# Last MLP: two blocks of k instead of one in the seven-product form, for the first pair of down chunks of each quarter

## The chip, the cores and the metric

The kernel runs on one core of one Trainium2 chip. Its engines work side by side, each through its own list of instructions in order, and wait for each other by semaphores: TensorE (PE; its weight loads are shown as PEld), VectorE (DVE), ScalarE (ACT), GpSimd (POOL), and SyncE (SP), which here issues the loads of weights. Matrix products are summed in PSUM, in banks of 128 x 512 fp32; all other tiles lie in SBUF. The metric is the device time of one execution in microseconds; less is better.

## The reference

Two layers, each a token mixer, a cross-attention to a memory and a squared-ReLU MLP, with plain residual adds, on 256 tokens of width 2048 in fp32. What matters here is the MLP of the second layer, the last one, which the final norm follows:

```python
D_MODEL = 2048; SEQ = 256; D_FF = 4 * D_MODEL

def squared_relu_mlp(h, w_up, w_down):
    return jnp.square(jax.nn.relu(h @ w_up)) @ w_down
...
x = x + squared_relu_mlp(rms_norm(x, g_ff[i]), f_w_up[i], f_w_down[i])
...
return rms_norm(x, g_final)
```

`w_up` is 2048 x 8192, `w_down` 8192 x 2048.

## The kernel before

Every fp32 operand of a large product is split into a high part (`hi`, rounded by ACT to the format that PE reads) and a low part (`lo`, the rest, by a subtraction on DVE); `split` does both. A product of two tiles is then three matmuls: high x high, low activation x high weight, high activation x low weight.

Weights come in tiles of two k tiles by 512 columns (128 x 1024 fp32 on chip, 512 KB). `wload` has SP load one into a ring of four raw tiles `wraw`; `wtile` splits it into a ring of three tiles `whi` and a ring of three `wlo` (pool `wp`). So casting and splitting can run ahead of PE by three tiles at most, loads by four raw tiles more.

The last MLP (`mlp` with `nxt.closing`) goes through four quarters of the 8192 hidden features. Each quarter `b` has an up stage, four chunks `n` of 512 features made by two calls of `gemm_feat` each (32 weight tiles in all); the result `r` (squared ReLU) is split into `hh` and `hl`. Then comes a down stage: 16 k tiles of the hidden features by the four chunks of 512 output columns. In the first three quarters chunks 0 and 1 are one pair, 2 and 3 another; in the last quarter only 0 and 1 are a pair, chunk 2 goes through `gemm_hid` and chunk 3 through `gemm_last`, which takes both buffers of the pool `act`.

A pair goes through `gemm_seven`. It sees four k tiles as a 2 x 2 block matrix: two blocks of two k tiles by two chunks, and on the other side two halves of 128 tokens by the two blocks of k. Instead of eight block products it makes seven, from sums and differences of blocks. Those of the weights are made by DVE (into `run`, and into one raw tile) and then split; those of the hidden features (`sums`) are made once a quarter by `token_sums` from the first up chunk, and serve both pairs. The remaining twelve k tiles, six weight tiles for each of the two chunks, are direct tiles: each is used for both halves of tokens, 12 matmuls. A product of the seven takes 6 matmuls. Direct tiles stand between the products (`whole`), so that DVE can keep up.

The four raw tiles of the block lie in a ring `ws` of four; the split parts of the four summed products lie in two tiles `own`, one high and one low, all other parts in the ring `whi`/`wlo`. The products go to four PSUM banks, (token half, chunk). Some of them are needed in two places: `keep` has ACT copy a bank to an SBUF tile `kept` while the bank goes on summing. These copies are `m5` and `m1` early, `u2` and `u3` later; `gather` adds them to `x` on DVE.

The order of instructions on each engine is fixed when the program is built: a scheduler follows the program order as priority and takes what it expects to be ready first. SBUF buffers of a pool are taken when free; a new tile waits for the last reader of the one before it.

Lines used below: 103 and 104 are the cast and the subtraction of `split`, 127 the load of `wload`, 174 and 179 the matmuls of `gemm_feat` (high and low weights), 190 and 191 its way out of PSUM, 649 the squared ReLU, 666 `gather`, 697 to 700 `token_sums`, 719 the loads of the block, 731 the matmul in `gemm_seven`, 763 `keep`, 771, 777, 782 and 787 the differences of weights, 791 the sum of `u3` and `m5`.

Of the kernel before, what the change touches and what calls it, by code (L numbers as in the profile page):

```python
# [9 lines left out]
F32 = mybir.dt.float32  # L10
F32R = mybir.dt.float32r
I32 = mybir.dt.int32
AF = mybir.ActivationFunctionType
ALU = mybir.AluOpType
AX = mybir.AxisListType

P = 128
D = 2048
S = 256
KT = D // P  # L20
NB = 512
NCH = D // NB
KB = 2
# [15 lines left out]
class Trunk:  # L39
# [454 lines left out]
    def attention(self, x, layer, cur, nxt):  # L494
        nc, a, tc = self.nc, self.a, self.tc
        wq, wk, wv, wo = (a[k][layer] for k in ("x_w_q", "x_w_k", "x_w_v", "x_w_o"))
        hT = cur.act
        with tc.tile_pool(name="at", bufs=2, reuse_waits="tile") as ap:
# [3 lines left out]
            memT = self.mem_prep(ap, layer)  # L502
# [44 lines left out]
            for hd in range(HEADS):  # L547
                q = proj(hT, wq, hd, "q")
                self.flush()
                k = proj(memT, wk, hd, "k", (1, 2, 3, 0))  # L550
# [6 lines left out]
            oT = self.new_act()  # L557
            homes = iter(("vh", "vl") * 2 + ("ql", "qh") * 6)
            ws = lambda: ap.tile([P, KB * NB], F32, name="ws", tag=next(homes))
# [6 lines left out]
            def values(h0):  # L566

                vs, more = [], {}

                def end(t, n, src):  # L570
                    if not vs:
                        vs.extend([ap.tile([P, 2, HD], F32R, name=nm) for nm in ("vh", "vl")] for _ in range(2))
                    part = more.pop((t, n), None)
                    if part is not None:
                        nc.vector.tensor_tensor(out=part, in0=src, in1=part, op=ALU.add)
                        src = part
                    vh, vl = (f[:, t, :] for f in vs[n - h0])
                    r = self.rstd_mem[:, t:t + 1]
                    nc.scalar.activation(out=vh, in_=src, func=AF.Copy, scale=r)
                    nc.vector.scalar_tensor_tensor(out=vl, in0=src, scalar=r, in1=vh.bitcast(F32),  # L580
                                                   op0=ALU.mult, op1=ALU.subtract)

                self.gemm_seven(tiles, token(memT), self.mem_sums, wv, h0, 0,
                                lambda t, n, part: more.update({(t, n): part}), end)
                return vs

# [35 lines left out]
                nc.vector.tensor_tensor(out=xc, in0=part, in1=xc, op=ALU.add)  # L622

            for j in range(0, NCH, 2):
                self.gemm_seven(tiles, token(oT), sums[0], wo, j, 0, gather)
                for n in (j, j + 1):
                    self.at(1 + n - j, lambda n=n: nxt.chunk(x, n))


    def mlp(self, x, layer, cur, nxt):  # L630
        nc, a, tc = self.nc, self.a, self.tc
        wu, wd = a["f_w_up"][layer], a["f_w_down"][layer]
        hT = cur.act
        with tc.tile_pool(name="ml", bufs=4, reuse_waits="tile") as mp:
            r2 = mp.tile([P, 32 if layer else 56], F32, name="r2", bufs=1)[:, 0:2]
            ws = lambda: mp.tile([P, KB * NB], F32, name="ws", bufs=4)
            run = lambda: mp.tile([P, KB * NB], F32, name="run", bufs=1)
            kept = lambda i: mp.tile([P, NB], F32, name="kept", bufs=4)
            self.fifth = None if nxt.closing else mp
            for b in range(DFF // D):  # L640
                hid = []
                for n in range(NCH):
                    h = mp.tile([P, 4, S], F32R, name="hh")
                    l = mp.tile([P, 4, S], F32R, name="hl")
                    rs = []
                    for i in range(2):
                        r = mp.tile([P, 2, S], F32, name="r", bufs=2)
                        self.gemm_feat(hT, wu, 2 * (NCH * b + n) + i, r)
                        nc.vector.scalar_tensor_tensor(out=r, in0=r, scalar=0.0, in1=r, op0=ALU.max, op1=ALU.mult)
                        self.split(h[:, 2 * i:2 * i + 2], l[:, 2 * i:2 * i + 2], r)  # L650
                        rs.append(r)
                    hid.append((h, l))
                    if nxt.closing and n == 0:
                        sums = self.token_sums(ws(), lambda: mp.tile([P, 4, 2, P], F32R, name="sums", bufs=2), *rs)
                if nxt.closing:
                    own = lambda: mp.tile([P, KB * NB], F32R, name="own", bufs=2)
                    nxt.room = lambda: mp.tile([P, 2, NB], F32, name="g", tag="ws", bufs=4)
                if b == 0:
                    rstd = cur.rstd()
                    nc.vector.tensor_tensor(out=r2, in0=rstd, in1=rstd, op=ALU.mult)  # L660
                if b == DFF // D - 1 and not nxt.closing:
                    nxt.start()

                def gather(t, n, part, cs=None):
                    xc = x[:, t, cs or slice(n * NB, (n + 1) * NB)]
                    nc.vector.scalar_tensor_tensor(out=xc, in0=part, scalar=r2[:, t:t + 1], in1=xc,
                                                   op0=ALU.mult, op1=ALU.add)

                for n in range(NCH):
                    end = b == DFF // D - 1  # L670
                    if nxt.closing and not (end and n >= NCH - 2):
                        if n % 2 == 0:
                            self.gemm_seven((ws, run, kept), lambda kt, t: [f[:, kt % 4, t * P:(t + 1) * P]
                                                                            for f in hid[kt // 4]],
                                            sums, wd, n, b * KT, gather, own=own)
                            if end:
                                nxt.start()
                    elif nxt.closing and end and n == NCH - 1:
                        self.gemm_last(hid, wd, n, b * KT, lambda t, acc: nxt.finish(x, t, lambda cs: gather(
                            t, n, acc[:, cs.start - n * NB:cs.stop - n * NB], cs)))  # L680
                        break
                    else:
                        acc = self.gemm_hid(hid, wd, n, b * KT)
                        for t in range(2):
                            gather(t, n, acc[:, t, :])
                    if end:
                        self.at(4 + n if nxt.closing and n < 2 else 1, lambda n=n: nxt.chunk(x, n))

            self.fifth = None
# [12 lines left out]
        self.split(sh, sl, s)  # L702
        return sh, sl

    def gemm_seven(self, tiles, token, sums, w, n0, k0, gather, end=None, own=None):

# [13 lines left out]
        def parts(src, own=None):  # L722
            hi, lo = (own() if own else self.wp.tile([P, KB * NB], F32R, name=nm) for nm in ("whi", "wlo"))
            self.split(hi, lo, src)
            return half(hi), half(lo)

        begun = set()

        def into(key, kts, left, hi, lo, end=False):
            out = banks[key]  # L730
            mm = lambda s, m, e: nc.tensor.matmul(out, s, m, start=key not in begun, stop=e, skip_group_check=True)  # L731
            for kk in kts:
                ah, al = left(kk)
                mm(ah, hi[:, kk, :], False)
                begun.add(key)
                mm(al, hi[:, kk, :], False)
            for kk in kts:
                mm(left(kk)[0], lo[:, kk, :], True)

        def block(key, t, i, src, end=False):  # L740
            into(key, range(KB), lambda kk: token(KB * i + kk, t), *parts(src), end)

        def summed(key, k, src, end=False):
            into(key, range(KB), lambda kk: [f[:, k, kk, :] for f in sums], *parts(src, own), end)

        todo = {j: list(range(2, KT // KB)) for j in range(2)}

        def direct(j, first):

# [18 lines left out]
        for i, j in ((0, 0), (0, 1), (1, 0), (1, 1)):  # L768
            fetch(i, j)
        run = run()  # L770
        v.tensor_tensor(out=run, in0=raw[0, 1], in1=raw[0, 0], op=ALU.subtract)
        summed((0, 1), 0, run, True)
        block((1, 0), 0, 0, raw[0, 0], True)
        m5, m1 = keep((0, 1), 0), keep((1, 0), 1)
        block((0, 0), 0, 1, raw[1, 0])
        whole(1, 1)
        v.tensor_tensor(out=run, in0=raw[1, 1], in1=run, op=ALU.subtract)
        summed((1, 0), 1, run, True)
        gather(0, n0, m1)
        u2 = keep((1, 0), 2)  # L780
        whole(1, 1)
        v.tensor_tensor(out=raw[0, 1], in0=raw[1, 1], in1=raw[0, 1], op=ALU.subtract)
        summed((1, 0), 2, raw[0, 1], True)
        gather(0, n0 + 1, u2)
        u3 = keep((1, 0), 3)
        whole(0, 0)
        v.tensor_tensor(out=run, in0=raw[1, 0], in1=run, op=ALU.subtract)
        block((1, 0), 1, 1, run)
        whole(1, 1)
        summed((0, 1), 3, raw[1, 1])  # L790
        v.tensor_tensor(out=u3, in0=u3, in1=m5, op=ALU.add)
        whole(0, 0)
        gather(1, n0 + 1, u3)
# [749 lines left out]
```

## Time and profile before

| | us |
|---|---|
| runs: median of 3 (lowest, highest) | 2790.95 (2790.82, 2792.07) |
| the profiled execution: its time | 2789.63 |
| its span, first to last instruction | 2787.9 |
| last MLP, first quarter: up stage begins | about 2083 |
| down stages of quarters 1 to 3: begin | 2170.5, 2344.4, 2518.2 |
| last quarter: pair begins, and `gemm_hid` after it | 2692.1, 2734.3 |

All times of the profile are counted from its first instruction. A share of busy time is an average over stages with different limits, so the stages are read one by one: the chain of work that ended last shows, step by step back from the end, what each step waited for; the view by stretches gives each engine's busy time between two points of time; the waits show which engine waited for which, and for how long; the timeline gives single instructions (start, length, engine, line, operation, output and inputs, and in brackets the idle time before it with what ended it). The length that is shown for a matmul is longer than the distance to the next one, because matmuls overlap.

### The profile page before, as it was taken

How to read it: one execution, taken by the hardware profiler on the slowest of the kernel's cores; microseconds unless marked ns; L12 is line 12 of the kernel's file. 1: busy time of each engine (PE TensorE's matmuls, PEld its weight loads, DVE VectorE, ACT ScalarE, POOL GpSimd, SP SyncE). 2: the span in 40 equal slices, each digit the busy share in tenths (PEclk: the TensorE clock that was granted, in tenths of full speed). 3: DMA queues.
4: the chain of work that ended last, by engine and by line, in shares of the span. 5: the costliest groups of instructions: out<-in, count | busy, mean ns of one | idle time of the engine just before them, and what ended most of it. 6: DMA issues, size and time to landing. Idle time of an engine off the chain costs nothing. (4 is left out here: it accounts for less than half of the span.)

```text
span 2787.9 us, 39690 instructions
## 1 busy us (share of the span) xinstructions
PE 2767.1 (99%) x15020; PEld 2331.6 (84%) x15020; DVE 1984.8 (71%) x2740; ACT 1396.2 (50%) x1805; POOL 234.4 (8%) x435
## 2 busy tenths in 40 slices
PE   9999999999999999999999999999999999999998
PEld 7888888888888888888887888888888888888887
DVE  6865756778978778787567657557776767667665
ACT  6545544554534434444556445445554545445454
POOL 0100000001022222221213100000000000000000
PEclk9999999999999999999999999999999999999999
DMA  8766655557788888887879767564556566565655
GB/s 294 232 209 217 200 179 181 175 158 244 211 260 260 255 259 262 257 259 226 240 242 270 217 199 239 176 191 159 179 158 216 170 212 204 164 221 167 213 187 158
DMA packets 196223, 593.76 MB, mean 213 GB/s; under 512 B 45120, under 2 KB 47216, under 8 KB 195520
## 3 DMA queue, kind: packets, MB, share of 16 engines
q1 hardware_dynamic: 151728, 531.17, 60.7%
q0 software_dynamic: 43776, 59.01, 7.8%
q8 instruction: 117, 1.92, 0.3%
q10 hardware_dynamic: 528, 1.06, 0.1%
q14 instruction: 74, 0.61, 0.1%
HBM read 567.51 MB, written 23.46 MB: 212 GB/s over the span
## 5 line engine op out<-in xcount | busy, mean ns | idle before, releaser
L104 DVE TENSOR_TENSOR wlo<-wraw,whi 128x1024 fp32r<-128x1024 f32 (+1 forms) x893 | 1085.9, 1221 | 490.4 <-ACT whi L103 484.8
L103 ACT CAST whi<-wraw 128x1024 fp32r<-128x1024 f32 (+1 forms) x893 | 937.3, 1052 | 857.0 <-PE acc L731 204.5
L174 PE MATMUL acc<-act,whi 128*128 128x512 f32 x3072 | 742.4, 392 | 0.6 <-ACT whi L103 0.6
L174 PEld LDWEIGHTS acc<-act,whi 128*128 128x128 f32 x3072 | 562.7, 188 | 111.5 <-issue 2.6
L179 PEld LDWEIGHTS acc<-act,wlo 128*128 128x128 f32 x3072 | 394.9, 191 | 18.6 <-DVE wlo L104 2.9
L179 PE MATMUL acc<-act,wlo 128*128 128x256 f32 x3072 | 403.9, 283 | 1.9 <-DVE wlo L104 1.5
L159 PE MATMUL acc<-whi,act 128*128 128x512 f32 x1472 | 369.8, 393 | 6.2 <-ACT whi L103 5.4
L159 PEld LDWEIGHTS acc<-whi,act 128*128 128x128 f32 x1472 | 275.1, 189 | 64.0 <-ACT whi L103 5.4
L731 PE MATMUL acc<-whi,act 128*128 128x512 f32 x864 | 233.0, 392 | 0.0
L815 PE MATMUL acc<-whi,hl 128*128 128x512 f32 x544 | 213.3, 392 | 0.0
L814 PE MATMUL acc<-whi,hh 128*128 128x512 f32 x544 | 212.7, 391 | 0.0
L159 PE MATMUL acc<-wlo,act 128*128 128x512 f32 x736 | 197.9, 391 | 0.0
L731 PEld LDWEIGHTS acc<-whi,act 128*128 128x128 f32 x864 | 160.3, 188 | 36.5 <-ACT ends L763 1.9
L159 PEld LDWEIGHTS acc<-wlo,act 128*128 128x128 f32 x736 | 138.6, 188 | 28.9
L731 PE MATMUL acc<-whi,hh 128*128 128x512 f32 x378 | 148.4, 393 | 0.0
L731 PE MATMUL acc<-whi,hl 128*128 128x512 f32 x378 | 147.1, 389 | 0.0
L817 PE MATMUL acc<-wlo,hh 128*128 128x512 f32 x544 | 145.9, 390 | 0.0
L731 PE MATMUL acc<-wlo,act 128*128 128x512 f32 x432 | 133.1, 390 | 0.0
L815 PEld LDWEIGHTS acc<-whi,hl 128*128 128x128 f32 x544 | 102.1, 188 | 23.1 <-issue 2.2
L190 ACT COPY r<-acc 128x512 f32<-128x512 f32 x64 | 37.6, 587 | 166.7 <-PE acc L174 166.7
L817 PEld LDWEIGHTS acc<-wlo,hh 128*128 128x128 f32 x544 | 102.1, 188 | 21.5 <-issue 0.2
L814 PEld LDWEIGHTS acc<-whi,hh 128*128 128x128 f32 x544 | 102.1, 188 | 21.4 <-issue 0.4
(369 smaller groups left out, 2762.4 us busy)
## 6 DMA issues: line engine op xcount, KB each, us to landing
wraw<-in_f_w_up SPq DMA_DIRECT2D x256, 512.0 KB, 4.6
wraw<-in_f_w_down SPq DMA_DIRECT2D x228, 512.0 KB, 4.6
wraw<-in_x_w_q SPq DMA_DIRECT2D x64, 512.0 KB, 4.1
wraw<-in_x_w_k SPq DMA_DIRECT2D x64, 512.0 KB, 4.4
wraw<-in_b_w_out SPq DMA_DIRECT2D x64, 512.0 KB, 4.4
wraw<-in_a_w_in SPq DMA_DIRECT2D x63, 512.0 KB, 4.1
wraw<-in_x_w_v SPq DMA_DIRECT2D x48, 512.0 KB, 4.2
wraw<-in_x_w_o SPq DMA_DIRECT2D x48, 512.0 KB, 4.3
```

What stands on the lines that cost most here:

```text
L103: self.nc.scalar.copy(out=hi, in_=src)
L104: return self.nc.vector.tensor_tensor(out=lo, in0=src, in1=hi.bitcast(F32), op=ALU.subtract).ins
L159: nc.tensor.matmul(out[t], a[:, kt, sl], b[:, kk, :], start=st and a is ah, stop=en)
L174: nc.tensor.matmul(acc[:, f, :], hi[:, kk, sl], both[:, kt].rearrange("p a s -> p (a s)"), start=first and kk == 0, stop=last and kk == FK ...
L179: nc.tensor.matmul(acc[:, f, 0:S], lo[:, kk, sl], ah[:, kt, :], start=False, stop=last and kk == FK - 1, skip_group_check=True)
L190: nc.scalar.copy(out=dst, in_=acc[:, :, S:])
L731: mm = lambda s, m, e: nc.tensor.matmul(out, s, m, start=key not in begun, stop=e, skip_group_check=True)
L814: nc.tensor.matmul(acc[:, t, :], ah, hi[:, kk, :], start=kt == 0, stop=False)
L815: nc.tensor.matmul(acc[:, t, :], al, hi[:, kk, :], start=False, stop=False)
L817: nc.tensor.matmul(acc[:, t, :], hid[kt // 4][0][:, kt % 4, sl], lo[:, kk, :], start=False, stop=kt == KT - 1)
```

## The change

For the first pair of down chunks (`n == 0`) in each of the four quarters, `gemm_seven` takes two blocks of four k tiles in the seven-product form. Each of the seven products is followed by the same product of the second block, k tiles 4 to 7 of the quarter, into the same bank; the copies and additions after it are shared. The number of direct tiles falls from twelve to eight. The second pair stays as it was.

The four raw tiles of the second block are loaded by SP into a new tile `more` of the pool `act` (128 x 8 x 1024 fp32, the size of one activation tile), in program order after the third up chunk. Three differences of them are made by DVE after the fourth up chunk, and one more inside the pair (`t1`). A second set of `sums` is made after the second up chunk; the tiles `sums` become four instead of two. The parts of the second block all go through the ring `whi`/`wlo`. The copies of `keep` move from a ring of their own into the last quarter of `more`, in both pairs. The calls in the attention stages only pass `sums` as a list.

```diff
-            kept = lambda i: mp.tile([P, NB], F32, name="kept", bufs=4)
+            kept = lambda i: more[:, 6 + i // 2, i % 2 * NB:i % 2 * NB + NB]
...
                     if nxt.closing and n == 0:
-                        sums = self.token_sums(ws(), lambda: mp.tile([P, 4, 2, P], F32R, name="sums", bufs=2), *rs)
+                        sums = []
+                    if nxt.closing and n < 2:
+                        sums.append(self.token_sums(ws(), lambda: mp.tile([P, 4, 2, P], F32R, name="sums", bufs=4), *rs))
+                    if nxt.closing and n == NCH - 2:
+                        more = self.act.tile([P, 8, KB * NB], F32, name="more", tag="act")
+                        ahead = self.block_ahead(more, wd, b * KT)
+                if nxt.closing:
+                    ahead[-1]()
...
-                                            sums, wd, n, b * KT, gather, own=own)
+                                            sums, wd, n, b * KT, gather, own=own, ahead=ahead if n == 0 else None)
...
+    def block_ahead(self, tile, w, k0):
+        v = self.nc.vector
+        raw = {(i, j): tile[:, 2 * i + j] for i in range(2) for j in range(2)}
+        for (i, j), t in raw.items():
+            self.fed = self.nc.sync.dma_start(out=t.rearrange("p (k c) -> p k c", k=KB), in_=w[j, k0 // KB + 2 + i]).ins
+
+        def add():
+            v.tensor_tensor(out=tile[:, 4], in0=raw[0, 1], in1=raw[0, 0], op=ALU.subtract)
+            v.tensor_tensor(out=tile[:, 5], in0=raw[1, 1], in1=tile[:, 4], op=ALU.subtract)
+            v.tensor_tensor(out=raw[0, 1], in0=raw[1, 1], in1=raw[0, 1], op=ALU.subtract)
+        return raw, tile[:, 4], tile[:, 5], add
...
-        def block(key, t, i, src, end=False):
-            into(key, range(KB), lambda kk: token(KB * i + kk, t), *parts(src), end)
-
-        def summed(key, k, src, end=False):
-            into(key, range(KB), lambda kk: [f[:, k, kk, :] for f in sums], *parts(src, own), end)
-
-        todo = {j: list(range(2, KT // KB)) for j in range(2)}
+        def block(key, t, i, src, more=None):
+            into(key, range(KB), lambda kk: token(KB * i + kk, t), *parts(src))
+            if ahead:
+                into(key, range(KB), lambda kk: token(KB * (2 + i) + kk, t), *parts(more))
+
+        def summed(key, k, src, more=None):
+            into(key, range(KB), lambda kk: [f[:, k, kk, :] for f in sums[0]], *parts(src, own))
+            if ahead:
+                into(key, range(KB), lambda kk: [f[:, k, kk, :] for f in sums[1]], *parts(more))
+
+        todo = {j: list(range(4 if ahead else 2, KT // KB)) for j in range(2)}
...
+        far, t1, t2 = ahead[:3] if ahead else ({}, None, None)
         v.tensor_tensor(out=run, in0=raw[0, 1], in1=raw[0, 0], op=ALU.subtract)
-        summed((0, 1), 0, run, True)
-        block((1, 0), 0, 0, raw[0, 0], True)
+        summed((0, 1), 0, run, t1)
+        block((1, 0), 0, 0, raw[0, 0], far.get((0, 0)))
         m5, m1 = keep((0, 1), 0), keep((1, 0), 1)
-        block((0, 0), 0, 1, raw[1, 0])
+        block((0, 0), 0, 1, raw[1, 0], far.get((1, 0)))
         whole(1, 1)
         v.tensor_tensor(out=run, in0=raw[1, 1], in1=run, op=ALU.subtract)
-        summed((1, 0), 1, run, True)
+        summed((1, 0), 1, run, t2)
...
-        summed((1, 0), 2, raw[0, 1], True)
+        summed((1, 0), 2, raw[0, 1], far.get((0, 1)))
         gather(0, n0 + 1, u2)
         u3 = keep((1, 0), 3)
         whole(0, 0)
         v.tensor_tensor(out=run, in0=raw[1, 0], in1=run, op=ALU.subtract)
-        block((1, 0), 1, 1, run)
+        if ahead:
+            v.tensor_tensor(out=t1, in0=far[1, 0], in1=t2, op=ALU.subtract)
+        block((1, 0), 1, 1, run, t1)
         whole(1, 1)
-        summed((0, 1), 3, raw[1, 1])
+        summed((0, 1), 3, raw[1, 1], far.get((1, 1)))
```

More of the change, by code (lines that the diff above doesn't have):

```diff
@@ L581, in end @@
                                                    op0=ALU.mult, op1=ALU.subtract)
-                self.gemm_seven(tiles, token(memT), self.mem_sums, wv, h0, 0,
+                self.gemm_seven(tiles, token(memT), [self.mem_sums], wv, h0, 0,
                                 lambda t, n, part: more.update({(t, n): part}), end)
@@ L624, in attention @@
             for j in range(0, NCH, 2):
-                self.gemm_seven(tiles, token(oT), sums[0], wo, j, 0, gather)
+                self.gemm_seven(tiles, token(oT), sums, wo, j, 0, gather)
                 for n in (j, j + 1):
@@ L703, in token_sums, with gemm_seven @@
         return sh, sl
-    def gemm_seven(self, tiles, token, sums, w, n0, k0, gather, end=None, own=None):
+    def block_ahead(self, tile, w, k0):
[8 more added lines that the diff above has]
+        return raw, tile[:, 4], tile[:, 5], add
+    def gemm_seven(self, tiles, token, sums, w, n0, k0, gather, end=None, own=None, ahead=None):
         nc = self.nc
@@ L727, in gemm_seven, with into @@
         begun = set()
-        def into(key, kts, left, hi, lo, end=False):
+        def into(key, kts, left, hi, lo):
             out = banks[key]
```

## The prediction

> **What bounds the kernel now.** The page first: the span, then the busy shares.
>
> ```profile
> span 2787.9 us, 39690 instructions
> PE 2767.1 (99%) x15020; PEld 2331.6 (84%) x15020; DVE 1984.8 (71%) x2740; ACT 1396.2 (50%) x1805; POOL 234.4 (8%) x435
> ```
>
> TensorE (PE) is busy for all but 20.8 us. A share says nothing of one stage, so next comes the chain that ended last, for the down stages of the four quarters (start, length, matmuls).
>
> ```profile
> 2170.50 84.78 PE acc L731 x372
> 2344.35 84.79 PE acc L731 x372
> 2518.21 84.81 PE acc L731 x372
> 2692.08 42.42 PE acc L731 x186
> ```
>
> The chain through each down stage is matmuls and nothing else: 186 for one pair of chunks. Then busy time by stretch, in quarter two: the up stage, the first pair of down chunks, the second.
>
> ```profile
> 2257.10:2344.20 87.10, 87.10 (x505) 77.04 (x505) 58.41 (x63) 41.33 (x47) 0.00 (x0) 1.00 0.68 217
> 2344.20:2386.60 42.40, 42.40 (x187) 34.75 (x186) 32.27 (x32) 22.80 (x26) 0.00 (x0) 1.00 0.59 186
> 2386.60:2429.00 42.40, 42.40 (x188) 34.78 (x187) 28.08 (x28) 20.73 (x23) 0.00 (x0) 1.00 0.51 162
> ```
>
> Busy columns are PE, weight load, VectorE (DVE), ScalarE (ACT), GpSimd; then granted clock, DMA share, GB/s. PE is full in all three, at clock 1.00; DVE has 10.1 us free in the first pair. What PE still waits for in the last MLP, from the waits of 2083 to 2788:
>
> ```profile
> PEld acc L731 <- ACT kept L763: 3.4, 14, 0.3
> ...
> DVE ws L782 <- DMA ws<-in_f_w_down: 7.5, 6, 2.0
> ```
>
> Twice in each of seven pairs PE waits until ACT has copied a PSUM bank (`keep`). DVE waits for loads up to 2.0 us at a time, and no PE wait stands beside it. So PE issue sets the time, and a matmul removed is time removed if the parts still come early enough.
>
> **The price of a matmul.** From the PE timeline of quarter two:
>
> ```profile
> 2344.19 1.52 PE L731 MATMUL acc<-own,sums 128*128 128x512 f32 x6
> ...
> 2353.72 0.50 PE L731 MATMUL acc<-whi,hh 128*128 128x512 f32 x1
> 2354.06 0.39 PE L731 MATMUL acc<-whi,hl 128*128 128x512 f32 x1
> ...
> 2367.57 0.39 PE L731 MATMUL acc<-whi,hh 128*128 128x512 f32 x1
> ...
> 2386.61 1.52 PE L731 MATMUL acc<-own,sums 128*128 128x512 f32 x6
> ```
>
> Between 2367.57 and 2386.61 lie seven undisturbed direct tiles of 12: 84 matmuls in 19.04 us, 0.2267 us each, though one is shown as 0.39 long (they overlap). A product is 6, so 1.36 us. The pair took 2386.61 - 2344.19 = 42.42; 186 x 0.2267 = 42.16; the other 0.26 are the two `keep` waits (one at 2353.72: next matmul after 0.34 instead of 0.23).
>
> [...]
>
> **What goes.** Before: 7 products and 12 direct tiles, 7 x 6 + 12 x 12 = 186. After: 14 products (two blocks of k into the same banks) and 8 direct tiles, 84 + 96 = 180. Six fewer, in four quarters 24: 24 x 0.2267 = 5.44 us. The count is fixed by the code; no doubt of it is a rival.
>
> **The `keep` waits.** In the ACT timeline of quarter two:
>
> ```profile
> 2344.39 0.59 ACT L190 COPY r<-acc 128x512 f32<-128x512 f32 x1 [2.70 <-PE acc L174]
> 2345.82 1.05 ACT L103 CAST own<-run 128x1024 fp32r<-128x1024 f32 x1
> 2346.77 0.62 ACT L103 CAST hh<-r 128x512 fp32r<-128x512 f32 x1
> 2347.29 1.07 ACT L763 COPY kept<-acc 128x512 f32<-128x512 f32 x2
> 2348.24 2.02 ACT L103 CAST whi<-wraw 128x1024 fp32r<-128x1024 f32 x2
> ...
> 2352.14 1.06 ACT L103 CAST own<-ws 128x1024 fp32r<-128x1024 f32 x1 [1.88 <-PE acc L731]
> 2353.10 0.57 ACT L763 COPY kept<-acc 128x512 f32<-128x512 f32 x1
> ```
>
> and in the DVE timeline:
>
> ```profile
> 2357.41 1.22 DVE L104 TENSOR_TENSOR own<-ws,own 128x1024 fp32r<-128x1024 f32 x1
> 2358.56 0.68 DVE L791 TENSOR_TENSOR kept<-kept 128x512 f32<-128x512 f32 x1
> 2359.16 1.22 DVE L771 TENSOR_TENSOR run<-ws 128x1024 f32<-128x1024 f32 x1
> ```
>
> The copy `u2` starts at 2353.10, though its product ended near 2352.5: the cast of the next `own` part stood ahead of it, released only when PE was done with the high half of the previous one (2352.14). Afterwards the bank gets a second product of 1.36 us, so that cast (0.95 from start to start) is over before the bank is complete, and the copy (0.57) fits into the 1.36 us of the direct tile's first half. The same holds for `u3`, less surely: a ring cast released at the same point may stand in front. Left of the 0.26: between 0 and 0.26; I take 0.10. So the pair goes from 42.42 to 180 x 0.2267 + 0.10 = 40.90: 1.52 us in each quarter, 6.1 in all.
>
> **What is added, and its cover.** In the pair: 22 splits instead of 19 and one more subtraction (`t1`). At 1.22 (DVE) and 1.05 (ACT) that is 32.27 + 4 x 1.22 = 37.2 us of DVE and 22.80 + 3 x 1.05 = 26.0 of ACT, in 40.9 of PE. It fits, and back to back DVE starts one each 1.14 (2359.16 after 0.60, 2357.41 to 2358.56 1.15), so true load is nearer 35. But it is densest at the head, six products before the first direct tile: 8.2 us of PE. Counted from the first matmul of the pair, T: `own`, `t1` and raw[0,0] are ready (two ring slots are free ahead of PE, as raw[0,0] and raw[1,0] are now), and the third slot comes free at T. ACT in the 8.2 us: copy of r 0.5, cast of hh 0.5, two copies of banks 1.0, casts of four ring parts and one `own` 5 x 0.95: 6.7. DVE: three r operations 1.9, five splits 5.7: 7.6. Each ring cast is released by the third part before it, 1.1 us into that product (four matmuls), so raw[1,0] is cast from T + 2.4 to 3.5 and its low half written by T + 5.1; PE wants them at T + 5.4 and T + 6.4. The far raw[1,0] is cast from T + 3.8 to 4.9, its low half there by T + 6.2, wanted at T + 6.8 and T + 7.7. No stall, with 1.3 us or more to spare. From then on the 2.72 us direct tiles give DVE more than it needs. Taken: 0; bounds: 0, and 2.2 us per quarter (second rival).
>
> In the up stage: a second set of token sums (four operations of 128x256 and a split) and three subtractions.
>
> ```profile
> 2296.68 1.23 DVE L782 TENSOR_TENSOR ws<-ws 128x1024 f32<-128x1024 f32 x1 [1.91 <-DMA ws<-in_f_w_down]
> ...
> 2328.82 1.22 DVE L104 TENSOR_TENSOR wlo<-wraw,whi 128x1024 fp32r<-128x1024 f32 x1 [1.78 <-ACT whi L103]
> 2330.58 1.23 DVE L104 TENSOR_TENSOR wlo<-wraw,whi 128x1024 fp32r<-128x1024 f32 x1 [0.54 <-ACT whi L103]
> 2333.87 0.69 DVE L191 TENSOR_TENSOR r<-acc,r 128x512 f32<-128x512 f32 x1 [2.06 <-ACT r L190]
> ```
>
> The instructions on the tile `ws` (duration least, median, most; and of its loads, from issue to landing), and ten more microseconds by stretch:
>
> ```profile
> L699 DVE TENSOR_TENSOR ws<-r x4: 415/416/421, 2097.7 to 2619.0; 128x256 f32<-128x256 f32 x4
> ...
> DMA to landing us min/median/max: 3.5/5.5/8.1
> ```
>
> ```profile
> 2285.00:2295.00 10.00, 10.00 (x61) 8.86 (x60) 8.17 (x9) 4.93 (x7) 0.00 (x0) 1.00 0.92 320
> ```
>
> 4 x 0.42 + 1.22 + 3 x 1.22 = 6.6 us on DVE beside 58.41 of 87.10: hidden in idle gaps of 1.78 + 0.54 + 2.06 = 4.4 us in each pass over four weight tiles. If that cover were gone, it would cost up to 6.6 a quarter. The four loads (`block_ahead`, 512 KB each) move forward in SP's queue, ahead of the last eight up tiles' loads; nothing is loaded twice. 2.1 MB more in 87 us raises 217 GB/s to 241, and the queue ran at 320 in the ten microseconds of the last row with PE full. Were the up loads behind them late by all 6.6 us that 2.1 MB take at 320 GB/s, the four raw buffers still reach 4 x 2.78 = 11.1 us ahead (an up stage is 2518.21 - 2344.35 - 84.79 = 89.07 us for 32 tiles). Cost 0. Their target `more` lies in an activation buffer idle during the up stage, so SP does not wait there. `kept` in `more` costs nothing: its readers of the pair before are long done. The new argument lists in the attention stages change no instruction.
>
> **The sum.** The profiled execution is 2789.63 us: span 2787.9 and 1.7 around it. Less 6.1: span 2781.8, time 2783.5. The median of runs is 2790.95, 1.3 above the profiled one; the same 6.1 off gives **2784.9**.
>
> **Rivals.** (1) The `keep` waits stay 0.26: 5.44 us, 2785.5, just inside 0.2%. For it: they stand in all seven pairs; against: the cast ahead of the copy now starts a product earlier. (2) The dense head outruns ACT: its queue is in order, and if the copies m5 and m1 stand ahead of the casts of raw[1,0] and its far part, those wait for product four (T + 5.6), then two copies (1.0) and a cast (1.0): T + 7.6 for T + 5.4, 2.2 us in each quarter, 8.8 - 6.1 = 2.7 slower, 2793.7. For it: DVE and ACT are nearly full there; against: at 2347.29 the copies stand where their banks were ready, with casts ahead of them that were ready sooner. A milder form (0.5) gives 2786.9. [...] (3) Slower: the three subtractions stand in DVE's queue ahead of splits and their loads land late. Two of them wait for a load. If each load lands at 8.1 instead of 3.5, they wait 2 x 4.6 = 9.2; 4.4 are idle anyway, 4.8 reach PE in each quarter: 19.2 - 6.1 = 13.1 slower, 2804. It decides from a wait of 4.4 + 1.5 = 5.9 a quarter; the longest single wait now is 2.0, with PE unhurt. The loads are also issued some 20 us ahead.
>
> **How the numbers follow.** Forecast 0.58, (1) 0.17, (2) 0.18, (3) 0.07. About 0.2%, 5.6 us, is what a measurement can tell from no change: below 2785.4. The forecast is 0.5 us beyond that line, and the runs before spread from 2790.82 to 2792.07, so 0.08 of it and 0.14 of (1) count as same: faster 0.50 + 0.03 = 0.53; same 0.08 + 0.14 + 0.17 = 0.39; slower 0.07 + 0.01 = 0.08. The range runs from all waits gone (4 x (42.42 - 40.80) = 6.5, 2784.5) less 0.5 for the medians, 2784.0, to 2789.5, half of (2); left out are 0.09 of (2) and (3), 0.16.
>
> **What would show it.** In the chain, 366 matmuls for each of the first three down stages, 180 for the last; the first pair about 40.9 us, the second 42.4 as now. The `keep` waits should fall from 14 towards 6. A PE wait on `whi` or `wlo` within 10 us of T proves (2); DVE waits on `more` over 2 us in the up stage with PE idle behind them, (3). Any stretch outside the first pairs that changes by a microsecond makes the prediction wrong in its ground.

## The result, and the profile after

| | before | changed |
|---|---|---|
| median of 14 runs each, side by side (lowest, highest), us | 2790.45 (2788.78, 2795.37) | 2785.20 (2784.24, 2787.76) |
| the profiled execution: time, span | 2789.63, 2787.9 | 2785.89, 2784.2 |
| a later set, median of 15 and 11 runs | 2790.93 | 2785.99 |

The ratio is 0.9981, with a 95% interval from 0.9974 to 0.9989: 3.1 to 7.3 us faster, 5.25 between the medians. The later set gives 0.9982 (0.9973 to 0.9991), 4.9 between the medians. The gain is real and small, and its size is better read from the trace.

The page of the changed kernel, its span and its busy shares:

```profile
span 2784.2 us, 39706 instructions
PE 2762.7 (99%) x14996; PEld 2327.2 (84%) x14996; DVE 2025.3 (73%) x2788; ACT 1412.2 (51%) x1821; POOL 234.4 (8%) x435
```

24 matmuls fewer (15020 before), 48 more operations on DVE and 16 on ACT, and PE still at 99%. The chain that ended last, in its four down stages (start, length, matmuls):

```profile
2172.10 83.49 PE acc L750 x366
2344.65 83.47 PE acc L750 x366
2517.19 83.46 PE acc L750 x366
2689.72 41.10 PE acc L750 x180
```

Line 750 is what was line 731. The last row is a first pair by itself: 41.10 us, where it was 42.42, so 1.32 us less. The other stages are shorter by 1.29 to 1.35. The second pairs and the later up stages have not moved: from one down stage's end to the next one's start there are 2344.65 - 2172.10 - 83.49 = 89.06 us, where it was 2344.35 - 2170.50 - 84.78 = 89.07.

Four times 1.32 is 5.28 us, and the span fell by only 3.7. The rest is found at the start of the last MLP, in the chain of the changed kernel from 2076 to 2100:

```profile
2080.14 1.83 PE acc L174 x8
...
2084.76 6.21 DMA more<-in_f_w_down
...
2091.05 0.52 DVE more L719
...
2092.20 0.49 DVE act L246
...
2092.73 3.25 PE acc L174 x13
```

and in the same view of the kernel before:

```profile
2079.04 1.83 PE acc L174 x8
...
2090.96 3.43 PE acc L174 x15
```

(By these rows the up stage of the first quarter begins at 2079.04 in the kernel before, earlier than the 2083 of the table.) Two things are to be seen. The first up stage begins 1.10 us later in this execution; up to that point both programs issue the same work, so this is the spread between executions (last section). And the chain now passes through a load of the second block, the first of the three differences on DVE (line 719) and only then the last activation tiles (line 246) that PE needs. From its first row to the down stage this stage takes 2172.10 - 2080.14 = 91.96 us, where it was 2170.50 - 2079.04 = 91.46: 0.5 longer. So 5.28 - 0.5 - 1.1 = 3.7, which is the span.

Waits from 2080 to 2735 in the changed kernel (who waited for whom: us in total, times, longest):

```profile
DVE more L719 <- DMA more<-in_f_w_down: 14.6, 4, 4.7
...
PEld acc L750 <- ACT more L786: 3.3, 14, 0.2
...
PEld acc L750 <- DVE wlo L104: 0.9, 4, 0.2
...
PEld acc L174 <- DVE act L246: 0.6, 1, 0.6
```

The waits for `keep` (line 786 now) are still 14: the prediction saw them fall towards 6. Two kinds are new: PE waits once in each quarter for a low part, and DVE waits for each quarter's loads, up to 4.7 us. In the first quarter that wait is the shortest, 0.90 us at the start of the up stage, and only there does PE wait behind it (last row). In the other three the first difference stands in the second pair of the quarter before, at 2238.57, 2411.59 and here, some 17 us before that pair ends:

```profile
2584.16 1.23 DVE L719 TENSOR_TENSOR more<-more 128x1024 f32<-128x1024 f32 x1 [4.74 <-DMA more<-in_f_w_down]
```

### The profile page after: what moved, and what is told of

Same layout as the page of the kernel before. It is cut to its first block, busy times and chain, and to the rows that moved or that the text cites. A ratio compares the mean times of both kernels' runs of the same rounds, so it can differ in the third digit from the quotient of the medians.

```text
span 2784.2 us, 39706 instructions
## 1 busy us (share of the span) xinstructions
PE 2762.7 (99%) x14996; PEld 2327.2 (84%) x14996; DVE 2025.3 (73%) x2788; ACT 1412.2 (51%) x1821; POOL 234.4 (8%) x435
## 5 line engine op out<-in xcount | busy, mean ns | idle before, releaser
L104 DVE TENSOR_TENSOR wlo<-wraw,whi 128x1024 fp32r<-128x1024 f32 (+1 forms) x877 | 1066.8, 1221 | 437.4 <-ACT whi L103 432.1
L103 ACT CAST whi<-wraw 128x1024 fp32r<-128x1024 f32 (+1 forms) x877 | 920.6, 1051 | 825.1 <-PE acc L841 180.3
L841 PE MATMUL acc<-whi,hl 128*128 128x512 f32 x544 | 213.3, 392 | 0.0
L840 PE MATMUL acc<-whi,hh 128*128 128x512 f32 x544 | 212.7, 391 | 0.0
L750 PE MATMUL acc<-whi,hh 128*128 128x512 f32 x338 | 132.8, 393 | 0.0
L750 PE MATMUL acc<-whi,hl 128*128 128x512 f32 x338 | 131.6, 389 | 0.0
```

The source lines that it names most:

```text
L103: self.nc.scalar.copy(out=hi, in_=src)
L104: return self.nc.vector.tensor_tensor(out=lo, in0=src, in1=hi.bitcast(F32), op=ALU.subtract).ins
L840: nc.tensor.matmul(acc[:, t, :], ah, hi[:, kk, :], start=kt == 0, stop=False)
L841: nc.tensor.matmul(acc[:, t, :], al, hi[:, kk, :], start=False, stop=False)
```

## The experiments

In the expectations, A is my account: PE's issue sets the time, each product is worth 1.36 us, and what else is lost is in the three places just named. B is each time the rival that is described there.

### One product, put back and taken out

The first kernel is the changed one with one product's matmuls issued twice, so that the pair has 186 matmuls again.

```diff
-                into(key, range(KB), lambda kk: [f[:, k, kk, :] for f in sums[1]], *parts(more))
+                p = parts(more)
+                for _ in range(2 if k == 3 else 1):
+                    into(key, range(KB), lambda kk: [f[:, k, kk, :] for f in sums[1]], *p)
```

> The changed kernel, with the matmuls of the last product of the second block issued twice in the first pair of each quarter (that product is added twice; 6 matmuls more per pair, 186 as before the change; splits, loads and subtractions are those of the changed kernel). Theory A (PE issue sets the time of the pair, the added work of DVE and ACT is hidden): each first pair goes from 41.10 to 41.10 + 6 x 0.2267 = 42.46 us, the whole from 2785.2 to about 2790.6, as before the change. Rival B (the pair is set by DVE or ACT, so that matmuls have slack): the first pair stays within 0.5 us of 41.10 and the time within 2 us of the changed kernel.

Measured: 2791.13 us, median of 10 runs; the ratio to the kernel before is 1.0001 (0.9992 to 1.001). Its chain:

```profile
2174.23 84.83 PE acc L750 x372
...
2695.88 42.48 PE acc L750 x186
```

Six matmuls more make the pair 42.48 - 41.10 = 1.38 us longer (the other three stages grow by 1.32 to 1.37), and the whole gain is gone. The other side is the kernel before with the last product's six matmuls left out in the first pairs, without anything else of the change:

```diff
-        summed((0, 1), 3, raw[1, 1])
+        if own and n0 == 0:
+            parts(raw[1, 1], own)
+        else:
+            summed((0, 1), 3, raw[1, 1])
```

> The kernel before, with the six matmuls of the last of the seven products left out in the first pair of each quarter (that product is missing from the output; its splits stay). Theory A (the gain is the matmul count and nothing else): first pairs go from 42.42 to 42.42 - 1.36 = 41.06 us, 2790.5 - 5.4 = 2785.1, the time of the changed kernel. Rival B (part of the gain of the changed kernel comes from elsewhere, from fewer direct tiles or loads moved): first pairs at 41.3 or more.

Measured: 2784.24 us, median of 9 runs, ratio 0.9978 (0.9968 to 0.9987). Its chain:

```profile
2168.64 83.43 PE acc L731 x366
...
2686.19 41.09 PE acc L731 x180
```

180 matmuls take 41.09 us with twelve direct tiles and no second block, and 41.10 with the second block. So what the change adds inside the pair (three splits, a subtraction, parts that come through the ring) costs, on balance, next to nothing beside its matmuls, and the six matmuls are the gain of the pair. Both support A. (The small waits inside the two pairs are not the same: a little less for `keep` and 0.07 more for a low part, as the next two parts show.)

### The waits for `keep`

In the ACT timeline of the changed kernel, around the copy `u2` of quarter two:

```profile
2356.56 1.06 ACT L103 CAST own<-ws 128x1024 fp32r<-128x1024 f32 x1 [0.30 <-PE acc L750]
2357.92 1.06 ACT L103 CAST whi<-wraw 128x1024 fp32r<-128x1024 f32 x1 [0.30 <-PE acc L750]
2358.88 0.57 ACT L786 COPY more<-acc 128x512 f32<-128x512 f32 x1
```

and on PE:

```profile
2359.53 0.47 PE L750 MATMUL acc<-whi,hh 128*128 128x512 f32 x1
2359.84 0.39 PE L750 MATMUL acc<-whi,hl 128*128 128x512 f32 x1
```

The cast of `own` comes earlier than before, as the prediction had it. But then a ring cast for a direct tile, released by PE in the middle of the second product, stands in front of the copy. The copy ends at 2359.45; the direct tile's second half begins at 2359.53, and its next matmul follows at 2359.84, after 0.31 us where 0.2267 is the undisturbed distance. That is 0.085 lost, and the same once more at `u3`. The direct tile behind `u2` does not even write the bank that is copied: its second half writes (0, 1), the other bank of the same PSUM tile `acc`. So the next kernel pairs the banks in tiles by chunk, and puts behind each late copy (`u2`, `u3`) a direct tile of the other chunk; behind `u2` it stood already. The matmuls are the same; their order and the order of the last additions change.

```diff
+        if ahead:
+            banks = {(0, 1): acc[0][:, 0], (1, 1): acc[0][:, 1], (1, 0): acc[1][:, 0], (0, 0): acc[1][:, 1]}
...
         u3 = keep((1, 0), 3)
-        whole(0, 0)
+        whole(*((1, 1) if ahead else (0, 0)))
...
         block((1, 0), 1, 1, run, t1)
-        whole(1, 1)
+        whole(*((0, 0) if ahead else (1, 1)))
...
+        if ahead:
+            for j in (1, 0):
+                whole(j, 1 - j)
+                for t in (1 - j, j):
+                    gather(t, n0 + j, banks[t, j])
+            return
```

The first direct tile also moves from behind the third product to ahead of it.

> The changed kernel with the four banks of the first pair paired by chunk instead of crosswise in their two PSUM tiles, the first direct tile moved ahead of the third product, and two direct tiles exchanged, so that no direct tile writes to a tile from which a copy of keep is being read. Theory A (the 0.30 us that the first pair takes over 180 x 0.2267 = 40.80 are two waits for keep of 0.09 each, which stand because a cast of the weight ring sits in ACT's queue ahead of the copy, and one wait of 0.07 for a low part at the sixth product): first pairs of 40.80 to 40.90 us, no wait for keep in them, six left in the three second pairs. Rival B (the waits belong to the copies themselves, wherever they stand, or move to the ends of the pair): first pairs of 41.05 us or more.

Measured in a single execution: 2783.23 us. Its chain, first and last down stage, and its waits from 2165 to 2735:

```profile
2170.27 83.26 PE acc L750 x366
...
2687.26 40.87 PE acc L750 x180
```

```profile
PEld acc L750 <- ACT more L786: 1.4, 6, 0.2
...
PEld acc L750 <- DVE wlo L104: 0.9, 4, 0.2
```

The pair is 41.10 - 40.87 = 0.23 us shorter, and eight of the 14 waits are gone; the six left are those of the three second pairs. 40.87 is 180 x 0.2267 = 40.80 and 0.07 that stays. At `u2` the trace tells what did it. The direct tile there is the same as in the changed kernel, and the copy still stands behind a ring cast and still ends just before that tile's second half: it runs from 2356.83 to 2357.40, the second half begins at 2357.48, 0.08 later in both kernels. Yet the next matmul follows at 2357.71, after 0.23 us. Only the tile in which the written bank lies is another one, so at `u2` the pairing of the banks removed the wait. At `u3` the direct tile was exchanged as well, and there the two were not tried apart.

### The head of the pair

The 0.07 is the other new wait. From the DVE timeline of the changed kernel, quarter two, whose pair begins at 2344.49:

```profile
2348.38 1.22 DVE L104 TENSOR_TENSOR own<-run,own 128x1024 fp32r<-128x1024 f32 x1
2349.51 1.22 DVE L104 TENSOR_TENSOR wlo<-ws,whi 128x1024 fp32r<-128x1024 f32 x1
```

The second row is the low part of raw[1,0], for the fifth product (the expectations call it the sixth). It is ready at 2350.73, 0.1 before its turn at 2350.83, and PE loses 0.07 on it even so (the next product begins at 2351.36, 0.53 later, where two matmuls take 0.45). Ahead of it in DVE's queue stands the low half of an `own` part that PE doesn't need until the seventh product, after a direct tile. If that is right, there is no spare time in the head, and one more operation there must reach PE whole. The next kernel adds a subtraction of 128 x 1024 there, whose result nothing reads:

```diff
         summed((0, 1), 0, run, t1)
+        if ahead:
+            v.tensor_tensor(out=late_out, in0=far[0, 0], in1=late.bitcast(F32).rearrange("p a b -> p (a b)"),
+                            op=ALU.subtract)
```

> The changed kernel with one more subtraction of 128x1024 (1.22 us, result not used) on DVE in the head of each first pair, held there because it reads the hidden features that are split last; it stands right ahead of the split of raw[1,0]. Theory A (in the head DVE has nothing to spare any more: the sixth product already waits 0.07 us for a low part): first pairs go from 41.10 to 42.1 to 42.3 us. Rival B (1.3 us to spare, as the prediction worked out): first pairs stay at 41.1.

Measured in a single execution: 2790.8 us. The first pair of quarter two takes 42.05 us (from its first matmul at 2346.49 to that of the second pair at 2388.54), 0.95 more than in the changed kernel (2344.49 to 2385.59, 41.10); in the four quarters it takes 42.05 to 42.08, just under the 42.1 to 42.3 of A. In its DVE, ACT and PE timelines:

```profile
2351.52 1.21 DVE L799 TENSOR_TENSOR more<-more,hl 128x1024 f32<-128x1024 f32 x1
2352.66 1.22 DVE L104 TENSOR_TENSOR wlo<-ws,whi 128x1024 fp32r<-128x1024 f32 x1
```

```profile
2352.63 1.06 ACT L786 COPY more<-acc 128x512 f32<-128x512 f32 x2
```

```profile
2352.61 0.39 PE L750 MATMUL acc<-whi,hl 128*128 128x512 f32 x1
2353.75 0.51 PE L750 MATMUL acc<-whi,hh 128*128 128x512 f32 x1 [0.75 <-ACT more L786]
2354.09 0.63 PE L750 MATMUL acc<-wlo,hh 128*128 128x512 f32 x2
```

The low part was due at 2352.61 + 0.23 = 2352.84 and is ready at 2353.88: 1.04 late. PE loses 1.03 here (from 2352.61 to 2354.09 it issues two matmuls in 1.48, where two take 0.45), and it lost 0.07 in the changed kernel. So 0.96 of the added 1.14 (2352.66 - 2351.52) reached PE. The scheduler put one matmul of the direct tile ahead of it; the wait that is printed is that matmul's, for the two early copies on ACT, which end at 2353.69, 0.2 before the low part. So two results that PE needs come almost together here, and the chain of this run passes through the copies. Counted from the start of the pair they end 7.20 us in, exactly as in the changed kernel (2353.69 - 2346.49 and 2351.69 - 2344.49), so the added subtraction didn't delay them; what it delayed is the low part, which by itself would have held PE until 2353.88. The run shows that the head has no room for one more operation on DVE, and the 1.3 us to spare are out. It also shows that ACT is not far behind: in this order of matmuls PE could not have gone on before 2353.69 in any case.

### The loads at the start

SP issued the second block's loads long before the point where the program asks for them, since their target was free: in the first quarter from 2080.17, among the first up loads, in the others from 2228.87, 2401.41 and 2573.95, in the second pair of the quarter before. The next kernel holds them behind the up load that precedes them in the program.

```diff
+        with self.tc.issue_after(self.fed):
-        for (i, j), t in raw.items():
+            for (i, j), t in raw.items():
```

> The changed kernel with the four loads of the second block held in SP's queue behind the last load of the third up chunk; in the changed kernel they are issued up to 110 us earlier, in the stage before, and DVE waits for them up to 4.7 us. Theory A (in the first quarter this early wait delays the last activation tiles and costs PE 0.5 us at the start of the MLP; in the other quarters it is hidden): the start of the first down stage comes 0.5 us earlier against the end of the attention (2079.98 in the changed kernel to 2172.10 there, 92.12 us, becomes 91.6, as in the kernel before: 2078.87 to 2170.50, 91.63); up stages of the other quarters stay 89.07 us. Rival B (three subtractions in a row late in the up stage stall PE there): the other up stages grow by 0.5 us or more.

Measured in a single execution: 2785.66 us. Its chain:

```profile
2080.36 1.83 PE acc L174 x8
...
2171.80 83.47 PE acc L752 x366
2344.34 83.47 PE acc L752 x366
```

The first up stage takes 2171.80 - 2080.36 = 91.44 us, as in the kernel before (91.46); the 0.5 is gone. The next one takes 2344.34 - 2171.80 - 83.47 = 89.07: the loads are now issued 50 to 53 us into each up stage (53 to 77 us later than before, not 110) and the three differences stand in its last third, and nothing reaches PE. DVE has no wait for a load of `more` left.

How much the early loads cost was seen by running the changed kernel once more, as it is:

> The changed kernel itself once more, on the same chip as the run beside it. Both theories: down stages of 83.47 three times and 41.10, as in its first profile; about 2785.2, a ratio of 0.998 to the kernel before.

Measured: 2785.99 us, median of 11 runs, ratio 0.9982. Its chain:

```profile
2079.18 1.83 PE acc L174 x8
...
2083.79 7.02 DMA more<-in_f_w_down
...
2171.95 83.46 PE acc L750 x366
```

Here the first up stage takes 92.77 us, 1.3 more than before, and the chain again passes through a load of the second block, which took 7.02 us. The down stages are the same to 0.03. So this loss varies between executions, 0.5 in the one and 1.3 in the other; the rest of the change doesn't. The other profiled executions fit. Where nothing is loaded early (the kernel before, with or without the six matmuls, and the three kernels with held loads) the first up stage takes 91.44 to 91.49 us. Where they are loaded early, it follows the start of the first difference on DVE, which waits for its load (both counted from the start of the up stage):

| execution | first difference starts, us | up stage takes, us |
|---|---|---|
| both pairs (next part) | 10.51 | 91.57 |
| banks apart | 10.90 | 91.94 |
| changed kernel | 10.91 | 91.96 |
| extra product; extra subtraction | 11.06 | 92.10 |
| changed kernel again | 11.73 | 92.77 |

From some 10.4 us on, each tenth of a microsecond that the difference starts later makes the stage a tenth longer: what the load loses there reaches PE whole.

### Further in the same direction

If a product saves what it should, the second pairs can have the form too, with the second block loaded again after the first pair:

```diff
+                            if n:
+                                ahead = self.block_ahead(more, wd, b * KT, n)
+                                ahead[-1]()
...
-                                            sums, wd, n, b * KT, gather, own=own, ahead=ahead if n == 0 else None)
+                                            sums, wd, n, b * KT, gather, own=own, ahead=ahead)
```

> The changed kernel with the same eight-k-tile form in the second pair of the first three quarters too, its second block loaded into the same tile as the parts of the first pair come free. Theory A (a pair saves its six matmuls wherever it stands, if its loads come in time): second pairs go from 42.42 to about 41.1 us, three of them, 2785.2 - 4.0 = 2781.2. Rival B (the loads of the second block come too late, since their buffers come free only during the first pair, and DVE's queue waits for them): second pairs of 42.4 us or more, 2785 or more.

Measured: 2784.65 us, median of 11 runs, ratio 0.9981 (0.9972 to 0.999): the same as the change alone. A down stage takes 82.65 us instead of 83.47 (from 2170.44 to 2253.09, the end of the next row), so 0.8 of the 1.3 is there. What is missing stands in its chain and its waits:

```profile
2170.44 32.93 PE acc L753 x144
2211.78 41.31 PE acc L753 x180
```

```profile
PEld acc L753 <- DVE x L673: 1.9, 3, 0.7
```

PE waits at the start of the second pair for the additions to `x` (line 673) that free its PSUM banks: DVE has taken up differences for the second pair before them. So the time stands between the two theories; PE waits for these additions, and for a load only so far as DVE's queue does. The next kernel joins this with the new pairing of banks and, in first pairs, the held loads.

> The banks set apart, the loads of the first pair's second block held behind the third up chunk, and both pairs in the eight-k-tile form. Theory A (the three act in different places and add: first pairs 40.87 each, second pairs 40.9, the first up stage 0.5 shorter; with the banks apart a second pair also no longer waits for the last additions to x of the pair before, 0.24 in the run of both pairs): 4 x 0.23 + 0.5 + 3 x 1.5 = 5.9 us off the changed kernel, 2779.3. Rival B (DVE is now the bound of the second pairs, and waits move to it): second pairs of 41.3 or more, 2780.5 or more.

Measured: 2782.93 us, median of 5 runs, ratio 0.9968 (0.9956 to 0.9981), short of what was expected. The down stages take 82.06, 82.75, 82.14 and 40.89 us; PE and DVE at the worst place, the second pair of quarter two:

```profile
2385.52 1.65 PE L755 MATMUL acc<-own,sums 128*128 128x512 f32 x6 [0.78 <-DVE x L673]
```

```profile
2382.92 1.23 DVE L823 TENSOR_TENSOR more<-more 128x1024 f32<-128x1024 f32 x1
2384.06 1.40 DVE L673 SCALAR_TENSOR_TENSOR x<-acc,r,x 128x512 f32<-128x512 f32 x2
```

By its numbers this is nearer to the rival: second pairs of 41.2 to 41.9 us. But the first DVE row is `t1`, which the second pair doesn't need until late; the two additions behind it are what PE waits for. Whether DVE is full or only does things in the wrong order is decided by the last kernel. It holds that difference, and the one into `run` after the first direct tile, each behind the addition to `x` that comes last before it in the program (for `run` that is the end of the first pair, for `t1` one of its own pair):

```diff
-            v.tensor_tensor(out=t1, in0=far[1, 0], in1=t2, op=ALU.subtract)
+            with held():
+                v.tensor_tensor(out=t1, in0=far[1, 0], in1=t2, op=ALU.subtract)
...
+        held = lambda: self.tc.issue_after(self.behind) if ahead and n0 else nullcontext()
+        with held():
+            v.tensor_tensor(out=run, in0=raw[1, 1], in1=run, op=ALU.subtract)
```

(`self.behind` is the last addition issued by `gather`.)

> The kernel of the three steps together, in which the second pairs took 41.2 to 41.9 us, with two of DVE's subtractions in each second pair (the second difference of the near block, and t1) held behind additions to x that come before them in the program. Theory A (the second pair starts late because DVE does those two, which nobody needs yet, ahead of the additions that free its first PSUM bank: 0.78 us in quarter two): second pairs of 40.9 to 41.0, 3 x 0.5 = 1.6 us off the time of the three together in the profile (span of the last MLP's down stages 287.84 becomes about 286.3). Rival B (DVE is simply full there, and the delay moves to a split): second pairs stay at 41.3 or more.

Measured: 2780.39 us, median of 5 runs (2776.33 to 2782.06), ratio 0.9959 (0.9945 to 0.9972). Its chain and its waits:

```profile
2172.11 81.69 PE acc L755 x360
2342.86 81.69 PE acc L755 x360
...
2684.39 40.90 PE acc L755 x180
```

```profile
PEld acc L755 <- DVE wlo L104: 0.9, 4, 0.2
```

360 matmuls at 0.2267 are 81.61 us, and the stages take 81.69: the only PE wait of the down stages is the 0.07 in each first pair's head. This version is 10.5 us faster than the kernel before, twice the change's gain, with seven pairs in the new form instead of four. By stage lengths it is 10.8 (296.80 to 285.98 us in the four down stages). The next engine to fill is DVE, busy for 37.9 of 41.0 us in this stretch, the last 37.1 of which belong to a first pair:

```profile
2339.00:2380.00 41.00, 41.00 (x190) 34.11 (x189) 37.89 (x37) 25.73 (x28) 0.00 (x0) 1.00 0.63 204
```

## Why the prediction came out as it did

- **PE issue bounds the stage, six matmuls a pair: right.** Predicted 5.44 us in all. Taking six matmuls out of the old pair made it 42.42 - 41.09 = 1.33 us shorter, putting six into the new one made it 1.38 longer, where 6 x 0.2267 = 1.36.
- **"Left of the 0.26: between 0 and 0.26; I take 0.10": this term failed.** It was worth 4 x 0.16 = 0.64 us, and is the distance from 5.44 to the 6.1. The cast of `own` does come earlier, as the step says; but its doubt, "a ring cast released at the same point may stand in front", held for `u2` as well as `u3`. By the distances between matmuls the wait at `u2` was 0.13 (2353.25 to 2354.06, 0.81 for three where three take 0.68) and is 0.085; that at `u3` was 0.085 (2357.94 to 2358.25) and stayed so. So the two fell from 0.21, a little less than the 0.26 that the prediction put down to them, to 0.17: 0.04 a pair where 0.16 was counted on, and the next point took that up. The rival with 5.44 us is what the pairs did, to 0.16. The waits could be removed, but by the banks and order, not by what the step named.
- **"No stall, with 1.3 us or more to spare" in the head: right as a cost, wrong as a margin.** The cost was 0.07 a quarter. The high half of raw[1,0] was cast from 2347.59, 3.1 us after the start and not 2.4, and DVE took the low half of `own` first, so the low half of raw[1,0] came at 6.2 us for 6.3, where the prediction had 5.1 for 6.4. The sum of DVE's work was right; its order was not thought of. The second rival (the head outruns an engine) was one operation away, on DVE, with ACT's copies ending only 0.2 us earlier.
- **Up stage, "cost 0": right in three quarters, 0.5 to 1.3 us wrong in the first.** The step that failed is that the loads go "ahead of the last eight up tiles' loads", "some 20 us ahead": SP issued them 53 to 77 us earlier than that place, so that the differences came early in DVE's queue too, where they waited up to 4.7 us for loads that take 6.2 to 7.5. In three quarters this happened in the second pair of the quarter before, where DVE has time to spare (28.08 us busy of 42.40 in the kernel before), and PE saw nothing of it. At the start of the first up stage, where the activation tiles are still being made on DVE, waits of 0.90 us and, in the repeat, 1.72 were enough. This is the third rival's mechanism, at a price of 0.5 to 1.3 where 19.2 was set, since it reached PE in one quarter instead of four, and not where the prediction looked for it. By the prediction's own sign (a stretch outside the first pairs that changes by a microsecond) its ground failed for this one stage in the repeat; every other stretch kept its length.
- **The sum.** 5.28 from the pairs less 0.5 to 1.3 is 4.0 to 4.8 us by the traces; the medians gave 5.25 and 4.9. 6.1 was too much by 1.3 to 2.1 of the traces, and all of it in the three terms above: the `keep` waits, the head and the first up stage. That the time came within 0.3 us of the forecast is in part luck: the gain of the medians was 0.8 less than forecast, and the kernel before came out 0.5 lower in the runs side by side (2790.45) than in the runs that the forecast started from (2790.95). The interval of the medians, 3.1 to 7.3, holds both 5.4 and 6.1 and so says little of the terms.

## What to carry to other kernels

Where TensorE's issue fills a stage, count its matmuls and check the stage's length in the chain, which repeats to some 0.05 us, before looking at whole times, which spread by several us. Then ask of every helper engine not whether its work fits but what stands ahead of the one result that TensorE wants next: a copy behind a cast, an addition behind a difference that nobody needs yet, a difference waiting for a load. Work that may start early should be held behind the work that frees a buffer; between the last two versions that alone was worth 1.9 us of stage lengths (287.84 to 285.98 in the four down stages), though it removes no instruction.

## What was not expected of the hardware

Before the last MLP the programs issue the same work, yet its first up stage begins anywhere from 2077.16 us (the old kernel less six matmuls) to 2082.13 (the changed one with a product twice) in the profiled executions, by the same row of the chain:

```profile
2077.16 1.83 PE acc L174 x8
```

```profile
2082.13 1.83 PE acc L174 x8
```

That is 5 us, as much as the change is worth. The traces show a part of the cause. In four of the eleven (the changed kernel, its repeat, the loads held, and the extra subtraction) the granted clock fell to 0.50 for 3.4 us in the middle of the program, at 1511 to 1513 us in three and at 1731 in the fourth; in the other seven it stayed at 1.00 there. The view by stretches for the changed kernel, and the same stretch of the kernel before (the third number from the end is the clock):

```profile
1511.20:1514.60 3.40, 3.38 (x8) 2.71 (x9) 3.37 (x7) 1.06 (x2) 2.55 (x5) 0.50 1.09 301
```

```profile
1511.20:1514.60 3.40, 2.88 (x13) 2.39 (x14) 3.37 (x8) 2.24 (x5) 2.37 (x4) 1.00 0.97 242
```

Eight matmuls that start at 1511.21 in the changed kernel last until the next ones at 1514.71, 3.50 us; in the kernel before the same eight take 1.94 (1511.72 to 1513.66). So some 1.5 us of a late start can come from there, more than the 1.10 between the two executions compared first. Where the rest comes from, and why the clock falls in some executions and not in others, no run here shows. This is why a single whole time could decide nothing in this study, and why the verdicts above rest on stage lengths.
